# Sums of squares of the norms over 1024 features added up on GpSimd instead of by matrix products

## The chip, the cores and the metric

The kernel runs on one core of one Trainium2 chip. The metric is the device time of one execution in microseconds (us). The kernel before took 1709.74 us, the median of three runs (1708.4 to 1711.4).

## The reference, cut to what matters

Two transformer blocks follow each other on 256 latent tokens with 1024 features, beside 256 context tokens. Every normalisation over the 1024 features divides a token by the root of its mean square, and is followed by a scale and a shift:

```python
def rms_norm(x, g):
    xf = x.astype(jnp.float32)
    y = xf * lax.rsqrt(jnp.mean(xf * xf, axis=-1, keepdims=True) + NORM_EPS)
    return (y * g.astype(jnp.float32)).astype(x.dtype)

for i in range(DEPTH):                                      # DEPTH = 2
    h_lat = modulate(rms_norm(x, norm_mix[i]), sh1, sc1)
    h_ctx = modulate(rms_norm(ctx, norm_mix[i]), csh1, csc1)
    ...                                                     # attention (i = 0) or latent attention (i = 1)
    x = x + g1 * y_lat
    x = x + g2 * squared_relu_mlp(modulate(rms_norm(x, norm_mlp[i]), sh2, sc2), mlp_w1[i], mlp_w2[i])
    if not last:                                            # the same for ctx
        ...
# second block
h = modulate_2(x, norm1_g[layer], sh1, sc1)                 # rms norm, scale, shift
...                                                         # gated delta rule, convolution, Fourier mix
x = x + g1 * mix
x = x + g2 * swiglu(modulate_2(x, norm2_g[layer], sh2, sc2), w_ffn_in[layer], w_ffn_out[layer])
return rmsnorm(x, final_g)
```

Everything is float32. The kernel makes eight such sums of squares over 256 tokens and one over 512 (latent and context together).

## The kernel before

**Tiling.** The latent `xl` and the context `xc` are kept transposed: 128 features on the partitions, 8 chunks of features (`KD`), 256 tokens. A product in full precision is three matrix products of split operands (`mm3`, lines 297 to 299: high by high, low by high, high by low). The weights come in blocks from DRAM on SP's queue, and each block is cut in two parts, `wh` on ScalarE (line 185) and `wl` on VectorE (line 186).

**Sum of squares.** Where a stage makes the last update of `x`, chunk by chunk, it also adds up the squares. `stat_open` clears a PSUM bank `part`. For chunk c, `stat_add` squares [128, 256] into `sq` (GpSimd, line 357; at the start of the kernel ScalarE, line 359). For the chunks 0 to 6 a product of `sq` with a [128, 32] matrix of ones adds the sum over the partitions into one of four strips of 32 rows of `part` (line 362). After chunk 6, VectorE copies `part` to `partS` (line 369), and small products with a selecting column (line 371) turn its strips into sums by token, in columns. Chunk 7 goes straight to the columns (line 365). Then VectorE scales the sum (`rq_m`, line 308), GpSimd raises it to the power of -0.5 (`rs`, line 310), and TensorE spreads `rs` over the partitions by a product (`R`, line 407 or 388). VectorE and ScalarE make the next stage's input `hh`, `hl` from `x` and `R` (lines 394 to 397).

**The places**, in order of time: the inputs (x and ctx); the last quarter of layer 0's out-projection, for the latent (`lat_norm`) and for the context; the end of layer 0's MLP (512 tokens wide, latent and context together); the end of layer 1's latent attention (`mla_out`); the end of layer 1's MLP; the end of the second block's mixing (`mix_out`); and the end of its MLP, before the output.

**Order.** Python generators emit the stages woven into each other (the out-projection of layer 0 beside attention, the context's delta rule beside layer 1), and a scheduler then puts each engine's instructions into one fixed order. The start of the kernel alone is in an order written out by hand. Each engine works through its own list, so an instruction that waits holds up all that is behind it on its engine.

Of the kernel before, what the change touches and what calls it, by code (L numbers as in the profile page):

```python
# [7 lines left out]
F32 = mybir.dt.float32  # L8
F32R = mybir.dt.float32r
I32 = mybir.dt.int32  # L10
AF = mybir.ActivationFunctionType
# [3 lines left out]
P = 128  # L15
# [25 lines left out]
def _const_arrays():  # L41
# [9 lines left out]
    sel = np.where(np.arange(128)[:, None] % 32 == 0, 1.0, 0.0).astype(np.float32)  # L51
    c1 = np.concatenate([ident, np.repeat(sel, 2, 1), np.ones((128, 32), np.float32), m0, m1, mb, _rope(64), _rope(32)], 1)
# [21 lines left out]
for _n, _w in (("ident", 128), ("sel", 2), ("ones", 32), ("m0", 128), ("m1", 128), ("mb", 64), ("rope64", 256), ("rope32", 128)):  # L74
    _C1[_n] = (_o, _o + _w)
    _o += _w
# [9 lines left out]
class Blank:  # L86
    """Stands for everything while the order of the weight blocks is recorded."""
# [17 lines left out]
class Split:  # L105
    """A float32 operand as two float32r parts: hi + lo is the value exactly."""
# [109 lines left out]
class Part:  # L216
    """Keys, queries and values of the delta rule on 256 tokens of the latent or the context."""
# [17 lines left out]
class Build:  # L235
# [9 lines left out]
    # -- debugging taps --  # L245
# [4 lines left out]
    # -- filler: work of the tensor engine that nothing waits for yet --  # L250
# [43 lines left out]
    # -- small pieces --  # L294
# [9 lines left out]
    def rsqrt_steps(self, out, ss, n, scale, eps=EPS):  # L304
        """out = (ss * scale + eps) ** -0.5 on [128, n]."""
# [7 lines left out]
    def cut(self, dst, src, scale=None):  # L313
        """dst.hi + dst.lo = src * scale, scale per partition."""
# [14 lines left out]
    def filled(self, gen):  # L329
        """Runs a generator, with as much filler as it yields."""  # L330
        for u in gen:
            self.fill(u)

    def stat_open(self, tag, n, bufs=2):
        """Begins the sums of squares of n halves of 256 tokens; column 2 r + t for token tile t of half r."""
        pool = self.ps_s if tag == "s" else self.ps_t
        part = pool.tile([P, 512], F32, tag=tag, name="part", bufs=bufs)
        self.nc.vector.memset(part, 0.0)
        if n == 1:
            ms = part[:, 256:260]  # L340
        else:
            ms = pool.tile([P, 4], F32, tag=tag, name="ms", bufs=bufs)
            self.nc.vector.memset(ms, 0.0)
        self.stat = (part, ms, n)
        return self.stat

    def stat_add(self, c, r=None, x=None, stat=None, sqp=None):
        """Adds chunk c of x (half r or both); the last one goes straight to the columns."""
        nc = self.nc
        part, ms, n = stat or self.stat  # L350
        rs = range(n) if r is None else (r,)
        f = slice(256 * rs[0], 256 * rs[-1] + 256)
        sq = sqp.tile([P, 256], F32, tag="sqf", name="sq", bufs=4) if sqp else self.tmp.tile([P, 512], F32, tag="sq", name="sq")
# [877 lines left out]
    def residual(self, c, ps, T, mod, g, last=False, r=None):  # L1231
# [4 lines left out]
        if last:  # L1236
            self.stat_add(c, r)
# [1021 lines left out]
```

## Time and profile before

| | before |
|---|---|
| median of 3 runs | 1709.74 us (1708.4 to 1711.4) |
| span of the profiled execution | 1706.0 us |
| TensorE busy | 1655.3 us, 97% of the span, 12256 products |
| VectorE busy | 1130.2 us, 66% |
| ScalarE busy | 715.1 us, 42% |
| GpSimd busy | 218.4 us, 13% |
| DMA moved | 257.31 MB, 151 GB/s on average |

The profiled execution has no device time of its own on record; its span is 3.7 us below the median of the runs. The busy shares are means over stages of different kinds. What a change is worth in a stage is read from that stage: from the order of the instructions in time, from how dense each engine is there, and from which wait ends last.

### The profile page before, as it was taken

How to read it: one execution, taken by the hardware profiler on the slowest of the kernel's cores; microseconds unless marked ns; L12 is line 12 of the kernel's file. 1: busy time of each engine (PE TensorE's matmuls, PEld its weight loads, DVE VectorE, ACT ScalarE, POOL GpSimd, SP SyncE). 2: the span in 40 equal slices, each digit the busy share in tenths (PEclk: the TensorE clock that was granted, in tenths of full speed). 3: DMA queues.
4: the chain of work that ended last, by engine and by line, in shares of the span. 5: the costliest groups of instructions: out<-in, count | busy, mean ns of one | idle time of the engine just before them, and what ended most of it. 6: DMA issues, size and time to landing. Idle time of an engine off the chain costs nothing.

```text
span 1706.0 us, 30446 instructions
## 1 busy us (share of the span) xinstructions
PE 1655.3 (97%) x12256; PEld 1405.4 (82%) x12256; DVE 1130.2 (66%) x2156; ACT 715.1 (42%) x1336; POOL 218.4 (13%) x294
## 2 busy tenths in 40 slices
PE   7999999999999999998999999999999999999998
PEld 5676687687877787666667999998989999899997
DVE  3575856667767776558777885675865856665643
ACT  3344443332332323147664644443533435444442
POOL 1430132110000000225321100101020000100000
PEclk8999999999999999999999999999999999999999
DMA  9684254225567777573222454454423545545652
GB/s 339 210 230 126 53 58 72 54 83 185 179 210 239 243 245 221 161 232 107 67 58 64 147 163 146 152 172 116 139 73 112 157 132 159 173 139 184 185 168 81
DMA packets 193229, 257.31 MB, mean 151 GB/s; under 512 B 9263, under 2 KB 166816, under 8 KB 193088
## 3 DMA queue, kind: packets, MB, share of 16 engines
q1 hardware_dynamic: 189488, 248.29, 46.1%
q0 software_dynamic: 2016, 2.33, 3.0%
q10 hardware_dynamic: 1584, 4.74, 0.8%
q8 instruction: 96, 1.57, 0.4%
q14 instruction: 45, 0.37, 0.1%
HBM read 254.28 MB, written 1.05 MB: 150 GB/s over the span
## 4 chain that ended last, share of the span: by engine, by line
PE 89%; DMA 4%; ACT 2%; DVE 2%; issue 1%; POOL 1%; POOLq 0%; DVEq 0%; SPq 0%; ACTq 0%
PE m L297 11%; PE m L299 11%; PE m L298 11%; PE ov L1091 3%; PE pf L297 3%; PE pf L298 3%; PE pf L299 3%; PE ip L297 2%; PE ip L298 2%; PE ip L299 2%; PE pps L1077 2%; PE adaps L508 2%; PE part L362 2%; PE ml L1534 1%; PE pg L299 1%; PE pg L297 1%
## 5 line engine op out<-in xcount | busy, mean ns | idle before, releaser
L185 ACT ACTIVATE wh<-wr 128x1024 fp32r<-128x1024 f32 (+3 forms) x354 | 332.2, 984 | 420.9 <-PE m L298 189.9
L186 DVE TENSOR_TENSOR wl<-wr,wh 128x1024 fp32r<-128x1024 f32 (+3 forms) x354 | 402.2, 1164 | 146.6 <-ACT wh L185 145.9
L299 PE MATMUL m<-hh,wl 128*128 128x256 f32 (+1 forms) x544 | 177.5, 329 | 0.5 <-DVE wl L186 0.5
L297 PE MATMUL m<-hh,wh 128*128 128x256 f32 (+1 forms) x544 | 176.7, 330 | 1.1 <-ACT hh L395 1.1
L298 PE MATMUL m<-hl,wh 128*128 128x256 f32 (+1 forms) x544 | 177.1, 328 | 0.0
L297 PE MATMUL m<-hidh,wh 128*128 128x512 f32 (+1 forms) x512 | 173.6, 341 | 0.0
L298 PE MATMUL m<-hidl,wh 128*128 128x512 f32 (+1 forms) x512 | 172.6, 338 | 0.0
L299 PE MATMUL m<-hidh,wl 128*128 128x512 f32 (+1 forms) x512 | 172.6, 338 | 0.0
L357 POOL TENSOR_TENSOR sq<-xl 128x256 f32<-128x256 f32 x48 | 31.6, 662 | 721.1 <-DVE xl L1234 692.5
L299 PEld LDWEIGHTS m<-hh,wl 128*128 128x128 f32 x544 | 103.3, 190 | 11.6 <-issue 1.9
L297 PEld LDWEIGHTS m<-hh,wh 128*128 128x128 f32 x544 | 102.3, 190 | 12.6 <-issue 1.9
L298 PEld LDWEIGHTS m<-hl,wh 128*128 128x128 f32 x544 | 103.4, 190 | 9.5 <-issue 0.8
L297 PEld LDWEIGHTS m<-hidh,wh 128*128 128x128 f32 x512 | 96.7, 190 | 15.5 <-issue 3.8
L298 PEld LDWEIGHTS m<-hidl,wh 128*128 128x128 f32 x512 | 97.1, 190 | 14.6 <-issue 4.8
L299 PEld LDWEIGHTS m<-hidh,wl 128*128 128x128 f32 x512 | 96.9, 189 | 13.3 <-issue 3.3
L297 PE MATMUL pf<-hfh,wh 128*128 128x256 f32 x352 | 99.5, 287 | 1.1 <-ACT hfh L395 1.1
L298 PE MATMUL pf<-hfl,wh 128*128 128x256 f32 x352 | 100.0, 285 | 0.0
L299 PE MATMUL pf<-hfh,wl 128*128 128x256 f32 x352 | 100.0, 285 | 0.0
L297 PE MATMUL ip<-wh,hh 128*128 128x256 f32 x288 | 86.2, 301 | 0.0
L298 PE MATMUL ip<-wl,hh 128*128 128x256 f32 x288 | 84.6, 294 | 0.2 <-DVE wl L186 0.2
L299 PE MATMUL ip<-wh,hl 128*128 128x256 f32 x288 | 83.6, 290 | 0.0
L1234 DVE SCALAR_TENSOR_TENSOR xl<-m,mod,xl 128x256 f32<-128x256 f32 x64 | 30.6, 481 | 74.3 <-PE m L299 74.2
(592 smaller groups left out, 4185.2 us busy)
## 6 DMA issues: line engine op xcount, KB each, us to landing
wr<-in_mlp_w SPq DMA_DIRECT2D x128, 512.0 KB, 4.6
av<-in_ada_w SPq DMA_DIRECT2D x48, 512.0 KB, 4.0
wr<-in_w_ffn_in SPq DMA_DIRECT2D x44, 512.0 KB, 4.6
wr<-in_w_in SPq DMA_DIRECT2D x42, 512.0 KB, 4.4
wr<-in_ada_w SPq DMA_DIRECT2D x32, 512.0 KB, 6.2
av<-in_w_mod SPq DMA_DIRECT2D x32, 512.0 KB, 4.1
wr<-in_w_gate SPq DMA_DIRECT2D x24, 512.0 KB, 4.6
wf<-in_ada_w SPq DMA_DIRECT2D x16, 512.0 KB, 11.6
```

Source lines behind the costliest of these rows:

```text
L185: b.nc.scalar.activation(out=hi[:, o + a:o + z], in_=t[:, a:z], func=AF.Copy)
L186: b.nc.vector.tensor_tensor(out=lo[:, o + a:o + z], in0=t[:, a:z], in1=hi[:, o + a:o + z], op=ALU.subtract)
L297: mm(ps, l.hi, r.hi, start=start, stop=False, **kw)
L298: mm(ps, l.hi, r.lo, start=False, stop=False, **kw)
L299: mm(ps, l.lo, r.hi, start=False, stop=stop, **kw)
L357: nc.gpsimd.tensor_tensor(out=d, in0=v, in1=v, op=ALU.mult)
L362: nc.tensor.matmul(part[j:j + 32, f], self.c1("ones"), sq[:, f], start=False, stop=c >= 3, skip_group_check=True)
L508: nc.tensor.matmul(ps[32 * j:32 * j + 32, :], S[:, k, :], m, start=k == 0, stop=k == KD - 1, skip_group_check=True)
L1077: nc.tensor.transpose(ps[:, o:o + P], pt[:, qt, k0:k0 + P], self.ident)
L1091: self.nc.tensor.matmul(o[64 * f:64 * f + 64, 0:256], vals(f, kt), T[f][:, kt, :], start=kt == 0, stop=kt == nk - 1, skip_group_check=True)
L1234: self.nc.vector.scalar_tensor_tensor(x, ps[:, 256 * i:256 * i + 256], mod[:, i, 8 * g + c:8 * g + c + 1], x, op0=ALU.mult, op1=ALU.add)
L1534: self.nc.tensor.matmul(s, q[:, i, t * P:t * P + P], k[:, i], start=True, stop=True)
```

## The change

All sums of squares over 1024 features are formed without the products of line 362.

- Each half has an accumulator `sqa` [128, 256] in SBUF. Chunk 0 is squared straight into it; the chunks 1 to 6 are squared into `sq` and added to `sqa` by GpSimd. Chunk 7 is squared into `sq`. Then two products per token tile with a column of ones, one of `sqa` and one of `sq`, give the sums by token. The clearing of PSUM, the copy `partS` and the selecting column go. The PSUM bank is taken only at chunk 7.
- The squares run on ScalarE in the out-projection of layer 0 (latent and context) and in `mla_out` (`act=True`), and on GpSimd in the three MLPs and in `mix_out`.
- For the two inputs, ScalarE squares the rows of tokens as they came from DRAM, 512 features at a time, and sums them along the row in the same instruction; VectorE adds the two halves of a row.
- Beside that, the constants lose the two columns of `sel`, the tiles of vectors are as wide as what they hold, and two small tiles of the latent attention share the tags of others.

```diff
-    def stat_open(self, tag, n, bufs=2):
-        pool = self.ps_s if tag == "s" else self.ps_t
-        part = pool.tile([P, 512], F32, tag=tag, name="part", bufs=bufs)
-        self.nc.vector.memset(part, 0.0)
...
+    def stat_open(self, tag, n, bufs=2, pool=None):
+        acc = [(p or self.tmp).tile([P, 256], F32, tag="sqa", name="sqa", bufs=1) for p in (None, pool)[:n]]
+        self.stat = {"tag": tag, "n": n, "bufs": bufs, "acc": acc, "ps": None}
         return self.stat
 
-    def stat_add(self, c, r=None, x=None, stat=None, sqp=None):
+    def stat_add(self, c, r=None, x=None, stat=None, act=False):
...
+        sq = None if c == 0 else self.tmp.tile([P, 512], F32, tag="sq", name="sq")
+        part = {r: acc[r] if c == 0 else sq[:, 256 * r:256 * r + 256] for r in rs}
         for r in rs:
-            v, d = (x or self.x[r])[:, c], sq[:, 256 * r:256 * r + 256]
-            if True and not sqp:
-                nc.gpsimd.tensor_tensor(out=d, in0=v, in1=v, op=ALU.mult)
+            v = (x or self.x[r])[:, c]
+            if act:
+                nc.scalar.activation(out=part[r], in_=v, func=AF.Square)
             else:
-                nc.scalar.activation(out=d, in_=v, func=AF.Square)
-        if c < KD - 1:
-            j = 32 * (c % 4)
-            nc.tensor.matmul(part[j:j + 32, f], self.c1("ones"), sq[:, f], start=False, stop=c >= 3, skip_group_check=True)
-        else:
+                nc.gpsimd.tensor_tensor(out=part[r], in0=v, in1=v, op=ALU.mult)
+            if 0 < c < KD - 1:
+                nc.gpsimd.tensor_tensor(out=acc[r], in0=acc[r], in1=part[r], op=ALU.add)
+        if c == KD - 1:
+            if st["ps"] is None:
+                pool = self.ps_s if st["tag"] == "s" else self.ps_t
+                st["ps"] = pool.tile([P, 512], F32, tag=st["tag"], name="part", bufs=st["bufs"])
+                st["ms"] = st["ps"][:, 256:260]
             for t in range(2 * rs[0], 2 * rs[-1] + 2):
-                nc.tensor.matmul(ms[:, t:t + 1], sq[:, t * P:t * P + P], self.c1("ones")[:, 0:1],
-                                 start=False, stop=True, skip_group_check=True)
-        if c == KD - 2:
-            sq = self.tmp.tile([P, 512], F32, tag="nm", name="partS")
-            nc.vector.tensor_copy(sq[:, f], part[:, f])
-            for t in range(2 * rs[0], 2 * rs[-1] + 2):
-                nc.tensor.matmul(ms[:, t:t + 1], sq[:, t * P:t * P + P], self.c1("sel")[:, 0:1],
-                                 start=False, stop=True, skip_group_check=True)
+                for i, y in enumerate((acc[t // 2], part[t // 2])):
+                    nc.tensor.matmul(st["ms"][:, t:t + 1], y[:, t % 2 * P:t % 2 * P + P], self.c1("ones")[:, 0:1],
+                                     start=i == 0, stop=i == 1)
...
         def tokens(i):
-            self.stats[i] = self.stat_open("s", 1)
             yield from self.load_T(self.x[i], xt[i])
-            for c in range(KD):
-                self.stat_add(c, 0, self.x[i], self.stats[i], self.wfirst)
-                yield 1.0
-            yield from self.half_R(i, R, self.stats[i])
+            ss = self.small.tile([P, 2, 2], F32, tag="nt", name="nt")
+            ms = self.small.tile([P, 2], F32, tag="nr", name="nr")
+            for q in range(2):
+                for t in range(2):
+                    sq = self.tmp.tile([P, 512], F32, tag="sq", name="sq")
+                    nc.scalar.activation(out=sq, in_=xt[i][t][:, 512 * q:512 * q + 512], func=AF.Square,
+                                         accum_out=ss[:, q, t:t + 1])
+                    yield 1.0
+                    if q and t:
+                        nc.vector.tensor_tensor(out=ms, in0=ss[:, 0], in1=ss[:, 1], op=ALU.add)
+                    yield 1.0
+            yield from self.half_R(i, R, {"ps": None, "ms": ms})
...
-            self.stat_add(c, 0, self.x[r], stat)
+            self.stat_add(c, 0, self.x[r], stat, True)
...
-                    self.stat_open(*(("s", 2) if l == 0 else ("fil", 1, 1)))
+                    self.stat_open(*(("s", 2, 2, mp) if l == 0 else ("fil", 1, 1)))
...
-            self.residual(c, ps, 256, self.mod1, 2, gr == 3)
+            self.residual(c, ps, 256, self.mod1, 2, gr == 3, act=True)
```

**Where the order of the instructions moves.** A row is one instruction, or a run of like ones, of one engine in its fixed order: line, operation, output and inputs, shape, count.

TensorE in layer 0's out-projection for the latent, at its end (`pps` turns the attention's weights, ScalarE copies them to `PT`, `ov` multiplies them with the values, `op` is the out-projection); before:

```order
L1077 MATMUL pps<-cst_81,Pm 128x128 x4
L1091 MATMUL ov<-PT,vB 64x256 x4
L362 MATMUL part<-sq,cst_81 32x256 x2
L1091 MATMUL ov<-PT,vB 64x256
L297 MATMUL op<-OTh,wh 128x256
L362 MATMUL part<-sq,cst_81 32x256
L1091 MATMUL ov<-PT,vB 64x256 x3
```

and after:

```order
L1076 MATMUL pps<-cst_81,Pm 128x128 x4
L1090 MATMUL ov<-PT,vB 64x256 x5
L296 MATMUL op<-OTh,wh 128x256
L363 MATMUL part<-cst_81,sqa 128x1
L1090 MATMUL ov<-PT,vB 64x256 x3
```

The two products with ones that stood between the fourth and the fifth product with `PT` are gone, and nothing stands in their place.

TensorE at the entry of layer 1 (`adaps` are products of the modulation, with weights just read from DRAM; `ms` are the columns of sums; `cq` is the first product that needs the norm); before:

```order
L508 MATMUL adaps<-wr,S_6421 32x512 x3
L362 MATMUL part<-sq,cst_81 32x512
L508 MATMUL adaps<-wr,S_6421 32x512 x3
L371 MATMUL ms<-cst_81,partS 128x1 x4
L365 MATMUL ms<-cst_81,sq 128x1 x2
L508 MATMUL adaps<-wr,S_6421 32x512 x2
L365 MATMUL ms<-cst_81,sq 128x1 x2
L508 MATMUL adaps<-wr,S_6421 32x512 x2
L407 MATMUL R<-cst_81,rs 128x128 x4
L508 MATMUL adaps<-wr,S_6421 32x512 x4
L297 MATMUL cq<-wh,hh 128x384
```

and after:

```order
L501 MATMUL adaps<-wr,S_6376 32x512 x6
L363 MATMUL part<-cst_81,sqa 128x1
L363 MATMUL part<-cst_81,sq 128x1
L363 MATMUL part<-cst_81,sqa 128x1
L363 MATMUL part<-cst_81,sq 128x1
L363 MATMUL part<-cst_81,sqa 128x1
L363 MATMUL part<-cst_81,sq 128x1
L363 MATMUL part<-cst_81,sqa 128x1
L363 MATMUL part<-cst_81,sq 128x1
L501 MATMUL adaps<-wr,S_6376 32x512 x6
L400 MATMUL R<-cst_81,rs 128x128 x4
L501 MATMUL adaps<-wr,S_6376 32x512 x2
```

All eight column products now stand ahead of the `adaps` that follow the first six, and six `adaps` instead of four stand between the first six and `R`.

VectorE at the end of `mix_out` (`xl` is the last update of x, `wl` the cut of the next weights, `nm` the first step that needs `R`); before:

```order
L1234 SCALAR_TENSOR_TENSOR xl<-wo,mod_116,xl 128x256 x2
L369 COPY partS<-part 128x256
L186 TENSOR_TENSOR wl<-wr,wh 128x1024
L308 TENSOR_SCALAR rq_m<-part 128x2
L186 TENSOR_TENSOR wl<-wr,wh 128x1024
L394 SCALAR_TENSOR_TENSOR nm<-xl,Af,R 128x256 x2
```

and after:

```order
L1233 SCALAR_TENSOR_TENSOR xl<-wo,mod_116,xl 128x256 x2
L185 TENSOR_TENSOR wl<-wr,wh 128x1024 x2
L307 TENSOR_SCALAR rq_m<-part 128x2
L387 SCALAR_TENSOR_TENSOR nm<-xl,Af,R 128x256 x2
```

`rq_m` now stands behind both cuts of weights, where one of them stood behind it before; the same holds at the entry of the second block.

## Rows read from the trace of the kernel before

**Rows 1.** Page, busy time of each engine, share of the span, instructions.

```profile
PE 1655.3 (97%) x12256; PEld 1405.4 (82%) x12256; DVE 1130.2 (66%) x2156; ACT 715.1 (42%) x1336; POOL 218.4 (13%) x294
```

**Rows 2.** Page, chain of work that ended last, by line.

```profile
PE m L297 11%; PE m L299 11%; PE m L298 11%; PE ov L1091 3%; PE pf L297 3%; PE pf L298 3%; PE pf L299 3%; PE ip L297 2%; PE ip L298 2%; PE ip L299 2%; PE pps L1077 2%; PE adaps L508 2%; PE part L362 2%; PE ml L1534 1%; PE pg L299 1%; PE pg L297 1%
```

**Rows 3.** Line 362, its products: count, then duration in ns, smallest, median, largest.

```profile
L362 PE MATMUL part<-sq,cst x126: 379/379/617, 12.5 to 1696.7; 128*32 128x256 f32 x112, 128*32 128x512 f32 x14
```

**Rows 4.** Timeline, PE, final MLP: start, duration, line, operation, count, [idle before, releaser].

```profile
1681.42 0.28 PE L298 MATMUL po<-hidl,wh 128*128 128x256 f32 x1
1681.63 0.62 PE L362 MATMUL part<-sq,cst 128*32 128x256 f32 x2
1682.18 0.38 PE L299 MATMUL po<-hidh,wl 128*128 128x256 f32 x1
1682.41 0.28 PE L297 MATMUL po<-hidh,wh 128*128 128x256 f32 x1
1682.53 0.28 PE L298 MATMUL po<-hidl,wh 128*128 128x256 f32 x1
```

**Rows 5.** Timeline, PE, last quarter of layer 0's MLP, 512 tokens wide.

```profile
718.01 0.39 PE L297 MATMUL m<-hidh,wh 128*128 128x512 f32 x1
718.33 1.04 PE L362 MATMUL part<-sq,cst 128*32 128x512 f32 x2
719.30 0.50 PE L298 MATMUL m<-hidl,wh 128*128 128x512 f32 x1
719.64 0.39 PE L299 MATMUL m<-hidh,wl 128*128 128x512 f32 x1
719.87 0.39 PE L297 MATMUL m<-hidh,wh 128*128 128x512 f32 x1
```

**Rows 6.** Timeline, PE, end of layer 0's out-projection for the latent.

```profile
332.17 0.63 PE L362 MATMUL part<-sq,cst 128*32 128x256 f32 x4
332.98 0.65 PE L1091 MATMUL ov<-PT,vB 128*64 128x256 f32 x2 [0.18 <-ACT PT L1082]
```

**Rows 7.** Windows: start:end, length, busy of PE, PEld, DVE, ACT, POOL, clock, DMA.

```profile
337.00:345.00 8.00, 8.00 (x59) 6.37 (x59) 6.82 (x17) 2.46 (x5) 3.74 (x6) 1.00 0.30 111
926.00:952.00 26.00, 24.46 (x206) 23.96 (x204) 23.96 (x61) 16.38 (x29) 3.30 (x3) 1.00 0.58 176
24.00:34.00 10.00, 7.61 (x38) 6.38 (x38) 7.06 (x19) 3.95 (x8) 0.69 (x1) 0.54 1.05 384
```

**Rows 8.** Timeline, PE, first product that needs the context's norm after the out-projection.

```profile
360.93 0.74 PE L297 MATMUL m<-hh,wh 128*128 128x256 f32 x4 [1.11 <-ACT hh L395]
```

**Rows 9.** Line 357, GpSimd's squares of the latent.

```profile
L357 POOL TENSOR_TENSOR sq<-xl x48: 608/612/1525, 323.6 to 1697.0; 128x256 f32<-128x256 f32 x48
```

**Rows 10.** Line 1173, GpSimd's sum of two tiles 512 wide.

```profile
L1173 POOL TENSOR_TENSOR bm<-bm,cst x8: 1082/1086/1107, 126.1 to 305.2; 128x512 f32<-128x512 f32 x8
```

**Rows 11.** Timeline, DVE and POOL, out-projection of the context.

```profile
344.67 2.16 POOL L357 TENSOR_TENSOR sq<-xc 128x256 f32<-128x256 f32 x2 [1.55 <-DVE xc L1227]
345.05 1.32 DVE L186 TENSOR_TENSOR wl<-wr,wh 128x1024 fp32r<-128x1024 f32 x1
347.04 1.21 DVE L186 TENSOR_TENSOR wl<-wr,wh 128x1024 fp32r<-128x1024 f32 x1
```

**Rows 12.** Timeline, PE, entry of layer 1.

```profile
729.87 1.05 PE L508 MATMUL adaps<-wr,S 128*32 128x512 f32 x4 [0.87 <-DMA wr<-in_w_mod]
...
733.24 1.90 PE L407 MATMUL R<-cst,rs 128*128 128x128 f32 x8
735.07 1.15 PE L508 MATMUL adaps<-wr,S 128*32 128x512 f32 x8
```

**Rows 13.** Timeline, end of mix_out.

```profile
1492.40 0.42 DVE L369 COPY partS<-part 128x256 f32<-128x256 f32 x1
...
1494.26 1.61 POOL L310 TENSOR_TENSOR rs<-rq_m,neghalf 128x2 f32<-128x2 f32 x1 [1.23 <-DVE rq_m L308]
```

**Rows 14.** Line 310, GpSimd's power of the norms' sums; duration in ns, smallest, median, largest.

```profile
L310 POOL TENSOR_TENSOR rs<-rq_m,neghalf x9: 695/714/1609, 19.7 to 1699.1; 128x2 f32<-128x2 f32 x8, 128x4 f32<-128x4 f32 x1
```

More of the change, by code (lines that the diff above doesn't have):

```diff
@@ L50, in _const_arrays @@
     mb = np.where((kc >= c0) & (kc < c0 + 16), 0.0, NEG).astype(np.float32)
-    sel = np.where(np.arange(128)[:, None] % 32 == 0, 1.0, 0.0).astype(np.float32)
-    c1 = np.concatenate([ident, np.repeat(sel, 2, 1), np.ones((128, 32), np.float32), m0, m1, mb, _rope(64), _rope(32)], 1)
+    c1 = np.concatenate([ident, np.ones((128, 32), np.float32), m0, m1, mb, _rope(64), _rope(32)], 1)
     le = (i <= j).astype(np.float32)
@@ L73 @@
 _o = 0
-for _n, _w in (("ident", 128), ("sel", 2), ("ones", 32), ("m0", 128), ("m1", 128), ("mb", 64), ("rope64", 256), ("rope32", 128)):
+for _n, _w in (("ident", 128), ("ones", 32), ("m0", 128), ("m1", 128), ("mb", 64), ("rope64", 256), ("rope32", 128)):
     _C1[_n] = (_o, _o + _w)
@@ L377, in stat_close @@
+    def stat_close(self):
+        n = 2 * self.stat["n"]
         rs = self.small.tile([P, 4], F32, tag="rs", name="rs")
-        a, z = (0, 2 * n) if r is None else (2 * r, 2 * r + 2)
-        self.rsqrt(rs[:, a:z], ms[:, a:z], z - a, 1.0 / D)
+        self.rsqrt(rs[:, :n], self.stat["ms"][:, :n], n, 1.0 / D)
         return rs
@@ L384, in half_R @@
         rs = self.small.tile([P, 4], F32, tag="rs", name="rs")
-        yield from self.rsqrt_steps(rs[:, 0:2], stat[1][:, 0:2], 2, 1.0 / D)
-        R[r] = stat[0][:, :256]
+        yield from self.rsqrt_steps(rs[:, 0:2], stat["ms"][:, 0:2], 2, 1.0 / D)
+        if stat["ps"] is None:
+            stat["ps"] = self.ps_s.tile([P, 512], F32, tag="s", name="part")
+        R[r] = stat["ps"][:, :256]
         for t in range(2):
@@ L399, in norm_R @@
     def norm_R(self, R):
-        n = 2 * self.stat[2]
+        n = 2 * self.stat["n"]
         yield 2.0
@@ L480, in turn @@
             nc.tensor.transpose(ps[:, :o], t[:o], self.ident[:o, :o])
-            d = self.const.tile([P, P], F32, name="vec" + rows[0][0])
-            nc.vector.tensor_copy(d[:, :o], ps[:, :o])
+            d = self.const.tile([P, o], F32, name="vec" + rows[0][0])
+            nc.vector.tensor_copy(d, ps[:, :o])
             for k, (a, z) in at.items():
@@ L673, in pair @@
                     yield 0.2
-        self.stats = {}
         with st, self.tc.manual_schedule():
@@ L1227, in outproj3, with residual @@
             self.nc.vector.scalar_tensor_tensor(x, ps, self.mod0[:, r, 16 + c:17 + c], x, op0=ALU.mult, op1=ALU.add)
-            self.stat_add(c, 0, self.x[r], stat)
+            self.stat_add(c, 0, self.x[r], stat, True)
             yield 0.7
-    def residual(self, c, ps, T, mod, g, last=False, r=None):
+    def residual(self, c, ps, T, mod, g, last=False, r=None, act=False):
         for i in range(T // 256) if r is None else (r,):
@@ L1236, in residual @@
         if last:
-            self.stat_add(c, r)
+            self.stat_add(c, r, act=act)
     def mlp(self, l, T, mod, head=None):
@@ L1494, in mla_heads @@
         kt = []
-        ss = self.small.tile([P, 4, 4], F32, tag="vs", name="vs")
-        rs = self.small.tile([P, 4, 4], F32, tag="vr", name="vr")
+        ss = self.small.tile([P, 4, 4], F32, tag="hn", name="vs")
+        rs = self.small.tile([P, 4, 4], F32, tag="hr", name="vr")
         for t in range(4):
```

13 lines of the change are left out of this document (2 added, 11 removed).

## The prediction

> **What bounds the kernel now.** I read the page first: TensorE is busy for 97% of the span and no other engine for more than 66% [rows 1]. The chain of waits followed back from the end runs mostly through products, and names line 362, the products with ones, with 2% of the span, about 34 us [rows 2]. So the removed products lie on the path, not beside it. The line's own view counts them: 126 records, two to a product, so 63 products: 56 over 256 tokens (seven in each of eight halves) and seven over 512 [rows 3]. What remains is what one of them costs in its stage, what becomes late in its place, and what the new work on ScalarE and GpSimd holds up.
>
> **The price of a product.** The timeline of the final MLP shows one in a dense stream. From the start of the product before it (1681.42) to the second product behind it (1682.41) pass 0.99 us; two steps of that stream are 2 x 0.12 = 0.24 [rows 4]. It costs 0.75 us, more than its own 0.62, since the products around it are spread. In the MLP 512 tokens wide, 718.01 to 719.64 is 1.63, less two steps of 0.23: 1.17 us [rows 5].
>
> **The sum, stage by stage**, on the clock of the profiled execution. Of the seven products of an MLP or of mix_out the seventh stands behind the last product of the stage, where the path runs through the last update of x and not through TensorE, so I count six there.
>
> *The inputs: 0.* 14 products go, but from 24 to 34 us the DMA engines are full (share 1.05) at half the clock, 0.54 [rows 7]: the first weights set the pace. The squares were ScalarE's before. Bounds: a loss of 1.5, if fewer products leave the clock low earlier (of that row's 7.61 us of products, some 3 us more at 1.2 instead of 2.4 GHz), and a gain of 2.
>
> *Out-projection, latent: 3.8.* Seven products are 5.3. But two of them stood between the products that wait for the attention's transposed weights: they end just before a product that still waits 0.18 us for the copy PT [rows 6]. In the new order nothing stands there, so that wait grows by what they filled, and two of the seven give nothing: 5 x 0.75 = 3.8. Bounds 3.0 and 5.3. The squares move to ScalarE, 31% busy in the next window [rows 7].
>
> *Out-projection, context: 5.3.* 7 x 0.75; TensorE has no gap there, 8.00 of 8.00 us [rows 7]. VectorE, at 6.82, is the next that could bind; the 1.1 us wait for this norm [rows 8] may go, since the sums stand earlier. I set these two against each other. Bounds 3.0 and 6.4.
>
> *MLP of layer 0: 7.8.* Six at 1.17 are 7.0. At the entry of layer 1, R started at 733.24, and the product that waits for weights from DRAM at 729.87 [rows 12]. Now all column products are ahead of that wait, so the norm is no longer late, and R waits for six adaps instead of four products with two columns and the late norm between. Four adaps take 1.15 us [rows 12]: six take 1.7, or 3.5 at half clock. R starts at 731.6 to 733.3, 0 to 1.6 earlier; I take 0.8. Bounds 6.0 and 9.5.
>
> *mla_out: 3.0.* 5.3 at full price. But behind it, from 926 to 952, VectorE is busy for 23.96 of 26 us, about as long as TensorE with 24.46 [rows 7]: products that come earlier wait there for cuts and for the convolution. The edit takes only a clearing and a copy from VectorE (0.42 for the copy, [rows 13]). I take a little over half. Bounds 1.0 and 5.3.
>
> *MLP of layer 1, mix_out, final MLP: 4.5 each, 13.5.* Six at 0.75. At the ends of the first two, rq_m falls behind a second cut of weights, 1.21 us [rows 11]. Against that, the copy of 0.42 is gone, and the power, which took 1.61 us beside that cut [rows 13], stands clear of it at 0.70 [rows 14]: 1.21 - 0.42 - 0.91 = -0.1, so R comes when it came. Bounds 3.5 and 5.3 each (the final one: 4.0 and 5.2).
>
> *New work.* GpSimd gets 48 additions of two tiles [128, 256]. The trace has none; the nearest rows are its square of that shape, 0.61 [rows 9], and its sum of tiles twice as wide, 1.08 [rows 10], so 0.54 to 0.61 us. In the three halves whose squares move to ScalarE one addition replaces one square, so GpSimd's load stays. In the others it does two operations a chunk, 1.2 us, where a chunk of an MLP's quarter or of mix_out is 24 products of 0.12 us [rows 4], 2.9 us; so only chunk 6's addition is near the end of a stage, and it is over before chunk 7 is there to be squared. I cost it at nothing. If that cover were gone, one addition, 0.6 us, would be added at each of four ends, inside the bounds.
>
> Sum: 0 + 3.8 + 5.3 + 7.8 + 3.0 + 13.5 = 33.4 us, the profiled span 1706.0 becoming 1672.6. The span is 3.7 us below the median of the runs; with that the time is 1709.74 - 33.4 = **1676.3 us**. The low bounds sum to -1.5 + 3.0 + 3.0 + 6.0 + 1.0 + 3.5 + 3.5 + 4.0 = 22.5 (1687.2), the high ones to 2 + 5.3 + 6.4 + 9.5 + 5.3 + 5.3 + 5.3 + 5.2 = 44.3 (1665.4).
>
> **Rivals.**
>
> *A. The woven halves give nothing.* In the two out-projections and in mla_out other engines take over as the bound: VectorE's 6.82 of 8 and 23.96 of 26 us speak for it [rows 7], the gapless 8.00 of 8 of TensorE against. Then 33.4 - 3.8 - 5.3 - 3.0 = 21.3 us are gained: 1688.4.
>
> *B. All comes out.* 42 products (all but the inputs') at 0.75 and seven at 1.17 are 31.5 + 8.2 = 39.7, and with the layer's entry (1.6), the context's wait (1.1) and the inputs (2) 44.4: 1665.3. The chain's 34 us for line 362, the inputs' products included [rows 2], speaks against most of it.
>
> *C. Slower, by GpSimd in VectorE's way.* Beside one cut wl, two squares took 2.16 us instead of 1.22, and the cut 1.32 instead of 1.21 [rows 11]. If an addition stretched to 1.08 held a cut that TensorE waits for by its whole length, 48 additions would cost 52 us and the kernel would take 1709.74 - 33.4 + 52 = 1728. It decides from 33.4 / 48 = 0.70 us per addition. Against it: of the two engines GpSimd is the one that was stretched, by 0.94, while the cut lost 0.11; 48 x 0.11 is 5 us if TensorE waited for each of them, and in dense stretches like [rows 4] it waits for none. The Trainium skill, "SBUF — State Buffer", section "Who interferes with whom", speaks against this change: GpSimd and VectorE share a port pair as an exclusive lock for a whole instruction, and the one that issues second blocks fully. The long squares agree with VectorE having been first; that rows show no cut blocked for a whole square agrees less. By that rule with every addition first, at 0.61 each, an estimate is 48 x 0.61 = 29 us lost, 1706: a gain of 4 left.
>
> *D. The products go but their time does not.* The order shows the 63 products gone and nothing of like size put in, so only waits could take it all: new ones of 33 us. Nothing in the profile names them.
>
> **How the numbers follow.** Forecast 0.67, A 0.14, B 0.11, C 0.05, D 0.03. About 0.2% (3.4 us) is what a measurement of this kernel can tell from no change. Forecast, A and B are faster by more: 0.92. D is within: 0.03. C is slower: 0.05. The range takes the forecast's bounds and the cases A and B: 1665 to 1689.
>
> **What would show it right or wrong.** The profile after should have no products with 32 columns of ones; TensorE's busy time should fall by about 35 us, with its share still near 97%. Between the places named, stretches should keep their length. Out-projection of the latent: a wait for PT of about 0.8 us. Entry of layer 1: R 1.7 to 3.5 us behind the product that waits for weights from DRAM, with its sums long there. Ends of layer 1's MLP and of mix_out: a power of 0.70 us with nothing beside it, and R as far behind the last product as before. From 926 to 952: if the norm of mla_out ends as long before the wait for the keys' norm as now, rival A holds there. GpSimd: additions near 0.6, up to 1.1 beside cuts. The prediction is wrong if VectorE's cuts become longer by some tenths throughout (C), if the first 40 us stretch by more than 2 us, or if the layers' entries show new waits for GpSimd's last addition.

## The result, and the profile after

The changed kernel takes **1685.86 us** (median of four runs, 1684.99 to 1686.62). Its ratio to the kernel before is 0.986, 95% interval 0.985 to 0.988: about 24 us faster, where the forecast was 33.4. The time lies inside the range of 1665 to 1689. The profiled span went from 1706.0 to 1683.2 us, by 22.8.

The page's busy times (beside [rows 1]): TensorE lost 30.9 us of busy time, where about 35 was forecast, and holds the same share, 97%; VectorE's time did not move; GpSimd got 37 us more.

```profile
PE 1624.4 (97%) x12114; PEld 1395.5 (83%) x12114; DVE 1131.8 (67%) x2139; ACT 723.3 (43%) x1360; POOL 255.3 (15%) x318
```

GpSimd's additions (line 355) and its powers (line 309; beside [rows 14]), durations in ns, smallest, median, largest:

```profile
L355 POOL TENSOR_TENSOR sqa<-sqa,sq x48: 723/743/1720, 325.2 to 1672.6; 128x256 f32<-128x256 f32 x48
...
L309 POOL TENSOR_TENSOR rs<-rq_m,neghalf x9: 696/707/1032, 16.5 to 1675.9; 128x2 f32<-128x2 f32 x8, 128x4 f32<-128x4 f32 x1
```

An addition takes 0.74 us by the median, and 17 of the 48 took 1.07 to 1.72 us; 0.54 to 0.61, and up to 1.1, was forecast. To see where the time went, take a VectorE instruction that both kernels have and read its start in both timelines: the difference is the gain up to there, and two such differences enclose a stage. The table holds such pairs.

| Up to | Start before | Start after | Gain so far | Of this stage | Forecast |
|---|---|---|---|---|---|
| end of layer 0's attention | 315.53 | 315.85 | -0.3 | -0.3 | 0 |
| out-projection, latent, to its norm's sum | 337.10 | 333.05 | 4.05 | 4.4 | 3.8 |
| out-projection, context | 427.58 | 417.93 | 9.65 | 5.6 | 5.3 |
| MLP of layer 0, body | 686.70 | 680.05 | 6.65 | **-3.0** | 0 |
| MLP of layer 0, end | 724.86 | 711.90 | 12.96 | 6.3 | 7.0 |
| entry of layer 1 | 789.55 | 777.82 | 11.73 | **-1.2** | 0.8 |
| mla_out | 987.81 | 976.23 | 11.58 | **-0.15** | 3.0 |
| MLP of layer 1 | 1217.21 | 1201.49 | 15.7 | 4.1 | 4.5 |
| opening of the second block | 1267.38 | 1253.12 | 14.3 | **-1.5** | 0 |
| mix_out | 1639.78 | 1621.27 | 18.5 | 4.2 | 4.5 |
| final MLP | 1694.29 | 1671.31 | 23.0 | 4.5 | 4.5 |

Wherever products were taken out of a dense stream, the forecast's size came. The missing 10.6 us lie mostly in the four bold rows: two stages in which the change removes nothing, and two in which the removed products had stood in waits.

**Where it went as forecast.** TensorE's timeline at the end of the latent's out-projection (beside [rows 6]): the wait for PT grew from 0.18 to 0.68 us.

```profile
329.58 0.65 PE L1090 MATMUL ov<-PT,vB 128*64 128x256 f32 x2 [0.68 <-ACT PT L1081]
```

GpSimd's and TensorE's timelines at the end of mix_out (beside [rows 13]): the power stands alone at 0.71 us, and R starts 4.30 us behind the last update of x, 4.07 before, because the norm's sum is read behind two cuts of weights now.

```profile
1476.67 0.71 POOL L309 TENSOR_TENSOR rs<-rq_m,neghalf 128x2 f32<-128x2 f32 x1 [2.36 <-DVE rq_m L307]
```
```profile
1477.43 0.71 PE L400 MATMUL R<-cst,rs 128*128 128x128 f32 x4 [2.24 <-POOL rs L309]
```

**mla_out.** Windows of this stage (columns as in [rows 7]): TensorE is idle for 1.5 of 6 us, and then the granted clock is 0.50 for 4 us and 0.77 for five more. Before, the stage's 15 us from 911 to 926 were all busy, at 1.00. The windows of before come first.

```profile
911.00:918.00 7.00, 7.00 (x52) 5.53 (x51) 6.13 (x14) 1.83 (x5) 1.84 (x3) 1.00 0.00 0
918.00:926.00 8.00, 8.00 (x46) 4.90 (x44) 5.04 (x12) 2.00 (x5) 2.53 (x4) 1.00 0.01 3
```

```profile
906.00:912.00 6.00, 4.50 (x27) 3.32 (x25) 4.83 (x9) 3.01 (x7) 2.30 (x4) 0.96 0.00 0
912.00:916.00 4.00, 3.87 (x19) 3.85 (x19) 3.77 (x6) 3.07 (x6) 0.00 (x0) 0.50 0.35 67
916.00:921.00 5.00, 5.00 (x36) 5.00 (x35) 2.00 (x6) 1.05 (x4) 0.00 (x0) 0.77 1.06 354
```

**Entry of layer 1.** TensorE's timeline (beside [rows 12]): two transfers of weights, not one, are waited for ahead of R; the four products of 717.00 (x8: two records to a product) run at half clock; and a third wait follows R.

```profile
717.00 3.19 PE L501 MATMUL adaps<-wr,S 128*32 128x512 f32 x8 [1.42 <-DMA wr<-in_w_mod]
721.14 1.05 PE L501 MATMUL adaps<-wr,S 128*32 128x512 f32 x4 [0.95 <-DMA wr<-in_w_mod]
722.12 1.16 PE L400 MATMUL R<-cst,rs 128*128 128x128 f32 x8
725.00 1.05 PE L501 MATMUL adaps<-wr,S 128*32 128x512 f32 x4 [1.72 <-DMA wr<-in_w_mod]
725.98 0.44 PE L296 MATMUL cq<-wh,hh 128*128 128x384 f32 x1
```

**Opening of the second block.** VectorE's, GpSimd's and TensorE's timelines, one after the other. The scheduler put vT ahead of A on VectorE; vT waited 0.54 us for si and then took 1.09 us (0.42 before), since GpSimd's AT, begun at 1224.44, held it up until 1227.82; and TensorE waited 1.61 us for E, which stands behind them. This wait is in all the kernels with the change. No run took it apart, so the reading of it as the cause of this stage's loss is argued from the rows alone.

```profile
1227.02 1.09 DVE L1679 SCALAR_TENSOR_TENSOR vT<-si,cv 128x256 f32<-128x256 f32 x1 [0.54 <-ACT si L1678]
1228.04 1.11 DVE L1832 SCALAR_TENSOR_TENSOR A<-kkp,bf,A 128x128 f32<-128x128 f32 x4
```
```profile
1224.44 3.38 POOL L1824 TENSOR_TENSOR AT<-AT,cst 128x1024 f32<-128x1024 f32 x1
```
```profile
1236.74 1.13 PE L1847 MATMUL Abp<-E,cst 128*128 128x512 f32 x2 [1.61 <-DVE E L1844]
```

### The profile page after: what moved, and what is told of

Read it like the earlier page. It is cut to its first block, busy times and chain, and to the rows that moved or that the text cites. A ratio compares the mean times of both kernels' runs of the same rounds, so it can differ in the third digit from the quotient of the medians.

```text
span 1683.2 us, 30197 instructions
## 1 busy us (share of the span) xinstructions
PE 1624.4 (97%) x12114; PEld 1395.5 (83%) x12114; DVE 1131.8 (67%) x2139; ACT 723.3 (43%) x1360; POOL 255.3 (15%) x318
## 4 chain that ended last, share of the span: by engine, by line
PE 87%; DMA 5%; DVE 4%; ACT 2%; issue 1%; POOL 1%; SPq 0%; POOLq 0%; DVEq 0%; ACTq 0%
PE m L296 10%; PE m L298 10%; PE m L297 10%; PE ov L1090 3%; PE pf L296 3%; PE pf L297 3%; PE pf L298 3%; PE ip L296 2%; PE ip L297 2%; PE ip L298 2%; PE pps L1076 2%; PE adaps L501 2%; PE ml L1533 2%; PE pg L298 1%; PE pg L296 1%; PE pg L297 1%
## 5 line engine op out<-in xcount | busy, mean ns | idle before, releaser
L185 DVE TENSOR_TENSOR wl<-wr,wh 128x1024 fp32r<-128x1024 f32 (+3 forms) x354 | 408.6, 1181 | 144.9 <-ACT wh L184 144.4
L544 DVE SCALAR_TENSOR_TENSOR acc<-av,S,acc 128x1024 f32<-128x1024 f32 x56 | 70.7, 1280 | 13.7 <-DMA av<-in_ada_w 13.5
```

Of the source, the lines that this page charges most:

```text
L185: b.nc.vector.tensor_tensor(out=lo[:, o + a:o + z], in0=t[:, a:z], in1=hi[:, o + a:o + z], op=ALU.subtract)
L544: op = eng.scalar_tensor_tensor(d, w, s, d, op0=ALU.mult, op1=ALU.add)
```

## The experiments

Each run stands beside runs of the kernel before on the same chip, so ratios are compared rather than times where two kernels ran in different groups. Stages are measured as in the table, by pairs of starts.

### The body of layer 0's MLP: where tiles lie

The change drops two columns (8 bytes a partition) from a constant tile, and the tiles allocated behind it start 32 bytes earlier. Two kernels move them alone. The first adds two unused columns to the changed kernel, which puts them back:

```diff
-    c1 = np.concatenate([ident, np.ones((128, 32), np.float32), m0, m1, mb, _rope(64), _rope(32)], 1)
+    c1 = np.concatenate([ident, np.ones((128, 32), np.float32), np.zeros((128, 2), np.float32), m0, m1, mb, _rope(64), _rope(32)], 1)
...
-for _n, _w in (("ident", 128), ("ones", 32), ("m0", 128), ("m1", 128), ("mb", 64), ("rope64", 256), ("rope32", 128)):
+for _n, _w in (("ident", 128), ("ones", 32), ("pad", 2), ("m0", 128), ("m1", 128), ("mb", 64), ("rope64", 256), ("rope32", 128)):
```

> The changed kernel with two columns of zeros put back into the table of constants (8 bytes a partition, which the allocator rounds to 32), so that every tile behind it lies on the same multiple of 64 bytes as in the kernel before; the order of the instructions of TensorE, VectorE and GpSimd is the same as in the changed kernel. Theory (placement): in the changed kernel's layer-0 MLP the products that read h step 0.233 us apart where they stepped 0.227 before, because the tiles moved by 32 bytes; here they step 0.227 again, about 3 us come back between 410 and 680 us, and the time is about 1682.7. Rival (something else of the change slows them, the order or GpSimd beside them): the steps stay at 0.233 and the time at 1685.9.

The second does the same to the kernel before with eight columns, 32 bytes, and changes nothing else; its order of instructions is that of the kernel before.

> The kernel before with eight columns of zeros more in the table of constants, so that all tiles behind it move by 32 bytes, onto the multiples of 64 that they have in the changed kernel; nothing else is changed. Placement: the products that read h in layer 0's MLP step 0.233 us apart instead of 0.227, and the time is about 3 us above 1709.7, some 1713. Rival: steps of 0.227 and 1709.7.

Groups by line and shape in the middle of this MLP (count, busy us, mean ns of one): before, before moved by 32 bytes, after, and after put back. The first line of each pair reads the MLP's input hh, the second the hidden tile.

```profile
L297 PE MATMUL m<-hh,wh 128*128 128x512 f32 x192 | 75.1, 391 | 0.0
...
L297 PE MATMUL m<-hidh,wh 128*128 128x512 f32 x194 | 76.1, 392 | 0.0
```
```profile
L297 PE MATMUL m<-hh,wh 128*128 128x512 f32 x192 | 76.3, 397 | 0.0
L297 PE MATMUL m<-hidh,wh 128*128 128x512 f32 x190 | 74.5, 392 | 0.0
```
```profile
L296 PE MATMUL m<-hh,wh 128*128 128x512 f32 x192 | 76.1, 396 | 0.0
...
L296 PE MATMUL m<-hidh,wh 128*128 128x512 f32 x193 | 75.5, 391 | 0.0
```
```profile
L296 PE MATMUL m<-hidh,wh 128*128 128x512 f32 x199 | 77.8, 391 | 0.0
...
L296 PE MATMUL m<-hh,wh 128*128 128x512 f32 x192 | 75.1, 391 | 0.0
```

A product that reads hh (or hl) takes 5 ns longer in the second and third kernel, and returns to 391 in the fourth; one that reads the hidden tile stays. There are 576 of the former (m from hh and wh, from hh and wl, from hl and wh, 192 each; hl is what the upper half hh leaves over): 576 x 5 ns is 2.9 us, and the stage lost 3.0 after the change, 3.0 in the moved kernel before, and nothing in the one put back (a gain of 7.8 going in, 8.1 coming out). In the eight profiles of kernels with the tiles moved the stage lost 2.9 to 3.0 us; in the four of padded changed kernels it gave between 0.0 and 0.7. So 32 bytes of placement is the cause. In the total time it is not resolved by these two runs: the moved kernel before took 1711.69 us beside 1713.05, ratio 0.9996 [0.998, 1.001], and the padded one 1685.04 us, ratio 0.9845 [0.983, 0.986] beside 0.986, both within the scatter.

Why the padded kernel's profile did not gain the 3 us in all lies at two other places. At the entry of layer 1 it lost 3.0 us, where the changed kernel lost 1.2. The other is seen in the windows of the out-projection, after and then padded: the low clock that follows the wait for the attention ended by 318 in one execution, and lasted into the next window in the other, which cost 2 us there. From 318 to 324 the granted clock was 0.73, 0.80 and 0.79 in three of the four padded kernels and 1.00 in the fourth, 0.83 in one kernel without padding and 0.90 to 1.00 in the rest; whether the placement has a part in it is open.

```profile
312.00:318.00 6.00, 5.19 (x30) 3.90 (x30) 3.66 (x12) 3.41 (x12) 0.00 (x0) 0.72 0.31 87
318.00:324.00 6.00, 6.00 (x46) 5.03 (x43) 4.70 (x16) 3.20 (x13) 0.00 (x0) 1.00 0.00 0
```
```profile
312.00:318.00 6.00, 5.78 (x28) 4.58 (x29) 3.32 (x10) 2.91 (x10) 0.00 (x0) 0.50 0.28 85
318.00:324.00 6.00, 6.00 (x33) 3.99 (x30) 3.54 (x12) 1.65 (x7) 0.00 (x0) 0.73 0.00 0
```

### mla_out: ScalarE, or waits that products had filled

Two theories stood. By one, the squares that the change puts on ScalarE hold up what ScalarE writes for TensorE there. This run leaves them on GpSimd:

```diff
-            self.residual(c, ps, 256, self.mod1, 2, gr == 3, act=True)
+            self.residual(c, ps, 256, self.mod1, 2, gr == 3)
```

> The changed kernel with the squares of mla_out on GpSimd again, as before, additions as in the change. Theory (ScalarE in the way): the squares stand between the cuts hch of the context's input on ScalarE; the product ba waits for hch and hcl (1.0 us in three waits near 907), TensorE idles 1.5 us of six, its clock falls to half from 912 to 918, and so the gain of this half is lost. Here these waits and the half clock go, and 2 to 3 us come back: about 1683. Rival (the removed products themselves had filled the time in which TensorE waits for the context's input, wherever the squares are made): idle time and half clock stay, 1686, or somewhat above if GpSimd with two operations a chunk makes the sum late.

Ratio 0.9856 [0.984, 0.987], 1686.83 us, as the change itself; the stage gave 0.2. Its windows show the same wait and the same fall of the clock, so ScalarE is not the cause:

```profile
906.00:912.00 6.00, 4.99 (x36) 4.16 (x34) 5.87 (x13) 1.67 (x4) 5.84 (x9) 1.00 0.00 0
912.00:916.00 4.00, 3.35 (x16) 2.97 (x16) 2.82 (x3) 2.56 (x4) 1.85 (x3) 0.54 0.00 0
```

By the other, the removed products had filled time in which TensorE waits, and kept its clock. This run puts seven products with ones back where they stood; nothing reads their result, and the norm is still made by the additions:

```diff
+            if c < KD - 1 and "idle" in st: nc.tensor.matmul(st["idle"][:32, :256], self.c1("ones"), part[r], start=True, stop=True, skip_group_check=True)
...
-            self.stat_open("s", 1)
+            self.stat_open("s", 1)["idle"] = self.ps_s.tile([P, 512], F32, tag="s", name="idle", bufs=2)
```

> The changed kernel with the seven products with ones of mla_out put back as well, their result unused (the sums still come from the additions). At the price of a dense stream they cost 7 x 0.75 = 5.3 us: 1691. If they only fill time in which TensorE waits and keep its clock up (the rival of e3), they cost nothing or gain: 1684 to 1686, with the clock near full from 912 to 918. If ScalarE's squares are the cause, the waits for hch and hcl stay and the time is 1688 to 1691.

```profile
906.00:912.00 6.00, 6.00 (x39) 4.15 (x38) 3.07 (x7) 3.02 (x7) 2.92 (x4) 1.00 0.00 0
912.00:916.00 4.00, 4.00 (x34) 3.96 (x34) 3.94 (x6) 3.36 (x6) 0.00 (x0) 1.00 0.35 81
```

TensorE is busy throughout at the full clock, 34 products pass from 912 to 916 where 19 did, and the stage gives 1.7 us. In the total time this run alone shows no gain: 1683.53 us, ratio 0.984 [0.982, 0.986], within the scatter of the changed kernel. The same with the tiles put back gave 1679.93, ratio 0.9805 [0.978, 0.983], and in a second run 1681.66, 0.982 [0.980, 0.984]:

> Both repairs in one: the changed kernel with the padded table of constants and the idle products in mla_out. If the two effects are independent, the layer-0 MLP keeps its steps of 0.227 (3 us) and mla_out its clock (2 to 3 us): 1680 to 1681, faster than both kernels. If the clock's fall depends on other things as well (it fell at one place of one execution for no reason that the order gives), 1682 to 1685.

> The padded table of constants and the idle products in mla_out, beside the changed kernel: 1680, 5 to 6 us below it, if both effects hold from one execution to the next; 2 to 3 below it if only one does.

Over all profiles the stage gave 1.7 to 3.3 us in the four with the unused products, and -1.2 to 0.2 in the six without (the additions on VectorE, below, left aside: -3.3). A single profile of this stage says little: e2 and e12, which keep the order of before here, show 1.7 and -3.2. The clock says more: it falls to 0.50 to 0.54 at this place in all seven profiles of changed kernels without the unused products, and in none of the four with them and the three with the order of before. In a stage that waits, seven products not only cost nothing: putting them back gained 2 to 3 us. GpSimd's additions hold up some of the cuts hcl there (0.91 and 0.95 us instead of 0.42), which TensorE waits for; with the additions on VectorE every hcl took 0.42, and TensorE still waited (0.80, 0.62 and 0.51 us) and fell to 0.50, from 918 to 920, so this is not the cause either. The changed kernel, run beside the last of them, kept both its own time and this window, 4.45 of 6 us busy and then 4 us at 0.50:

> The changed kernel once more, as the reference for the three beside it: 1685 to 1687. In a second profile the clock is at half near 912 to 918 again if the missing products are the cause there, and the products that read h in layer 0's MLP step 0.233 us apart again.

1685.15 us, ratio 0.984 [0.982, 0.986]: the padded kernel with unused products is 3.5 us below it on the same chip, where 5 to 6 was forecast if both effects hold and 2 to 3 if one does. The intervals of the two ratios overlap; of the times themselves, 1677.9 to 1683.9 and 1684.0 to 1685.7, none of one kernel reaches into the other's.

### The entry of layer 1

R stands behind products with weights from DRAM (adaps). This run gives R the bank that those use, so that the ones still to come stand behind R:

```diff
-        R[0] = self.ps_t.tile([P, 512], F32, tag="t", name="R")
+        R[0] = self.ps_t.tile([P, 512], F32, tag="fil", name="R", bufs=1) if n == 4 else self.ps_t.tile([P, 512], F32, tag="t", name="R")
```

> The changed kernel, with R of layer 1's entry in the PSUM bank that the adaps products use, so that all of these come behind the norm instead of ahead of R. Theory (adaps in the way): in the changed kernel R starts at 722.1, 5.2 us after its rs is done at 717.0, since six adaps stand ahead of it and wait twice for weights from DRAM (1.4 and 1.0 us), the four between at half clock. Here R starts within 0.5 us of rs, and 2 to 4 us are gained at cq; part of it is given back later, where the adaps stand in the stream of products (16 of them at some 0.3 us, 5 us less what they fill). Time 1683 to 1686. Rival (the weights from DRAM bound this entry whatever the order): cq starts no earlier relative to the last product of the MLP, 1686 to 1688.

R came at 718.04 instead of 722.12, and the gain stood 3.6 us higher at 740; by 790 all of it and 12 us more were gone. The weights' products, 4.0 us of waiting for DRAM among them, now stood alone behind it. 1696.78, ratio 0.991 [0.989, 0.993], is above both forecasts, 1683 to 1686 and 1686 to 1688. The waits for weights move with the order; they don't go.

The next run, on the padded kernel with the unused products, fills the wait instead: six more unused products with ones behind the column products.

```diff
         rs = self.stat_close()
+        for i in range(6 if n == 4 else 0): self.nc.tensor.matmul(self.stat["ps"][:32, 0:256], self.c1("ones"), self.stat["acc"][i % 2], start=True, stop=True, skip_group_check=True)
```

> The same with six products with ones, result unused, behind the column products at layer 1's entry; they also change the order there, to two adaps instead of six between the columns and R. Theory (the adaps that wait for weights stand in the way of R, and TensorE loses its clock while it waits): R starts 2 to 3 us earlier relative to the last product of the MLP, and, unlike in e5, the adaps follow at once behind R: 1677 to 1679. Rival (what R gains, cq loses again to the adaps behind it): 1680.

```profile
712.33 1.02 PE L502 MATMUL adaps<-wr,S 128*32 128x512 f32 x2 [1.42 <-DMA wr<-in_w_mod]
...
713.16 3.65 PE L397 MATMUL part<-sqa,cst 128*32 128x256 f32 x10
716.74 1.16 PE L401 MATMUL R<-cst,rs 128*128 128x128 f32 x8
717.83 0.64 PE L502 MATMUL adaps<-wr,S 128*32 128x512 f32 x4
```

Two products with weights (four records) stand ahead of R instead of six, one wait for DRAM is left, and the stage gives 1.5 us; it lost 2.9 in the same kernel without the six products, in one profile each. The time is **1674.83 us**, ratio 0.979 [0.976, 0.981], below both kernels, below the forecast of 1677 to 1679 and, with an interval that doesn't touch that of the changed kernel beside it, about 10 us faster. What the six products do is two things at once, a filled wait and another order around R; one run does not split them.

### The price in a dense stream, GpSimd's part, the inputs

Unused products put back in mix_out and the final MLP, seven each, by the line shown for mla_out:

> The changed kernel with seven products with ones, result unused, put back in mix_out and in the final MLP, where TensorE runs without a gap. The forecast's price for a product in a dense stream is 0.75 us, for six of each seven: 9.0 us, 1694.9. Rival (a product with ones costs its own time of 0.62 or less, and what the change gained here has another source, such as the clearing and the copy): 7 us or less, under 1693. Set beside the same seven products in mla_out, which cost nothing.

1694.82 us, ratio 0.990 [0.988, 0.992], beside 0.986 and 0.984 for the changed kernel: 7 to 10 us longer. The profiles agree: mix_out gave 0.0 instead of 4.2, and the final MLP 1.2 instead of 4.5, together some 7.5, where six each at 0.75 us are 9.0. The total time alone does not decide between the two theories, since the rival's 7 us lie within it; the starts around the products do, which are 0.74 us further apart for each of the twelve. In the final MLP the new order also moved ten of the twelve records of the output's transposes out of the stream, some 1.1 us, which is why it lost only 3.3. So [rows 4] priced these stages right, and the same products that are free in mla_out cost their full price here.

The 48 additions on VectorE instead of GpSimd:

```diff
-                nc.gpsimd.tensor_tensor(out=acc[r], in0=acc[r], in1=part[r], op=ALU.add)
+                nc.vector.tensor_tensor(out=acc[r], in0=acc[r], in1=part[r], op=ALU.add)
```

> The changed kernel with its 48 additions on VectorE instead of GpSimd. Theory of the forecast (the additions on GpSimd are covered, and what VectorE loses to them is small): no gain; VectorE has 48 instructions more, at about 0.4 us some 20 us of its time, and in the woven halves, where it is busy for over 0.85 of the time, it loses up to 1 us each: 1686 to 1689. Rival (GpSimd and VectorE block each other, rival C of the forecast): VectorE's cuts near the sums become shorter, and the time falls below 1684.

One takes 0.42 us there, not 0.74, and yet the time is 1688.51, ratio 0.987 [0.985, 0.988], against 0.986 and 0.984 for the two runs of the change: not better, and 2.7 us longer by medians. VectorE's cuts did get shorter, 402.5 us in all instead of 408.6, but the time did not fall with them. In its trace the stretch of the two out-projections gives 6.5 us instead of 10.0, where VectorE had no time left ([rows 7]), and mla_out loses 3.3. Moving the additions to VectorE gains nothing.

The kernel before with only the inputs' sums of squares made the new way:

> The kernel before with the new sums of the two inputs alone (rows of tokens squared and summed on ScalarE, 14 products fewer). The forecast sets this part at 0, since the first weights from DRAM set the pace: the same time as before within 1.5 us, and the first 100 us as long as before within what executions differ by. Rival (the products removed there were on the path, or the clock falls earlier without them): 2 us or more to either side.

1713.14 beside 1711.01, ratio 1.001 [0.999, 1.002]: nothing beyond the interval, where at most 1.5 us was forecast.

## Why the prediction was right, and where it was not

**Right.** The price of a product from its place in the stream: 4.5 forecast and 4.5 found in the final MLP, 4.5 and 4.2 in mix_out, 4.5 and 4.1 in layer 1's MLP, 7.0 and 6.3 at the end of layer 0's; and the run that put them back took 4.2 of 4.2 away in mix_out and 3.3 of 4.5 in the final MLP. That layer 1's MLP came so close is in part luck: over the profiles it gave 4.1 to 5.9, and 5.7 in the second one of the same kernel, above the bound of 5.3. The latent's out-projection gave 4.4 for 3.8, with the wait for PT grown as the step said (0.68; 0.8 forecast). The context's gave 5.6 for 5.3: its wait of 1.1 us for hh in [rows 8] is gone, a gain that I had set against VectorE, and a new wait of 0.4 us, for the latent's norm, stands at 338.90. The inputs gave nothing that a run of their own resolves.

**mla_out, 3.0 forecast, 0 found: the step that failed.** I put the loss behind the stage, at VectorE from 926 to 952, and left the stage itself at the full price of a dense stream. The loss lies inside it. The gain stood at 15.4 us at 922.86 in the trace of before, and fell to 12.3 by 932.39: TensorE had run ahead, waited for hch, hcl and baT, and then worked at half clock. For the latent's out-projection I asked what would stand in the products' place between two waits; here I did not ask it and took the stage for a dense one; no row of the prediction shows it, [rows 7] begin at 926. Its windows were full in the kernel before because the removed products filled them. Rival A is therefore true of this stage only, and for another reason than the one it gave; the two out-projections gave their 10 us.

**The entry of layer 1, 0.8 forecast, -1.2 found.** The six products ahead of R were counted right. The step took from [rows 12] that one transfer is waited for; the path came 11 to 13 us earlier at that point, and the products with weights as well, 10.5 to 13.9 us. What the step missed is that two waits, 1.42 and 0.95 us, with half clock between them, now stand ahead of R, where one of 0.87 us stood before; they took more than the earlier sums gave. In the two kernels that remove nothing near this entry, the moved one and the one with the inputs alone, it lost 2.3 and 2.8 us, so its price in one execution is known to 2 or 3 us only; the dense stages of the same kernels repeat within 0.6.

**Two terms that were not in the sum.** The 3.0 us of the MLP's body come from an edit that I read and costed at nothing: the two columns dropped from the constants. The 1.5 us at the second block's opening come, by the rows alone, from an order that the scheduler changed far from the edit; I had looked at the order only in the stages that the change touches.

**GpSimd.** An addition takes 0.74 us by the median, above the 0.54 to 0.61 that was worked out from other operations, and up to 1.72 beside a cut, where 1.1 was the most expected; two operations a chunk still fit in the 2.9 us of a chunk. Rival C fell by its price: the kernel is faster, and moving the additions away from GpSimd gains nothing. Its mechanism is there. VectorE's and GpSimd's timelines in mix_out after the change:

```profile
1468.34 1.61 DVE L185 TENSOR_TENSOR wl<-wr,wh 128x1024 fp32r<-128x1024 f32 x1 [0.49 <-ACT wh L184]
1469.88 1.76 DVE L185 TENSOR_TENSOR wl<-wr,wh 128x1024 fp32r<-128x1024 f32 x1
```
```profile
1468.95 1.60 POOL L355 TENSOR_TENSOR sqa<-sqa,sq 128x256 f32<-128x256 f32 x1
```

Such a cut takes 1.22 us alone, and an addition 0.74. The addition of 1468.95 takes 0.86 us more, which is how long the cut before it still ran (to 1469.95) less 0.14; the cut of 1469.88 takes 0.54 more, which is what the addition still had (to 1470.55) less 0.13. All 27 cuts of this width that began while GpSimd worked on whole tiles are longer in this way, by up to 1.86 us, and 17 were in the trace of before; the pair of rows by which the prediction doubted it was one of the mild ones. The Trainium skill, "SBUF — State Buffer", section "Who interferes with whom", has the second of two such instructions blocked until the first is done, and the trace agrees. What failed is the prediction's estimate from it, a gain of 4 us left where the change kept 24: it charged every addition to the path in full. In sum VectorE's cuts became longer by 6.4 us only, 402.2 to 408.6 on the two pages, because the squares of before had blocked some of them too and at least 14 additions are themselves the second, held up by a cut; and moving the additions to VectorE took the 6 us of cuts back without making the kernel faster.

Added up: -3.0 and -1.5 that were not foreseen, -3.15 in mla_out, -2.0 at the entry, and -0.9 in the remaining stages together make the 10.6 us between 33.4 and 22.8. By the number alone rival A's 1688.4 is nearer to 1685.86 than the 1676.3 that was forecast, but A lost it at the out-projections, which came at full price, so its nearness is luck. That the time lies inside the range, near its upper end, owes as much to the width of the range as to the sum.

## What to carry to other kernels

Price a removed product from the starts around it, but only where the stream is dense without it; where it fills a wait, ask what TensorE will do instead, because it then waits and loses its clock, and unused work can be worth its place. Compare the addresses of all tiles and the order far from the edit as well as near it: a constant shortened by 8 bytes cost 3.0 us, and one exchanged pair of VectorE instructions, by the rows, 1.5. A stage that waits for weights from DRAM can give back what comes early. Work moved from TensorE to GpSimd takes turns with VectorE's cuts: price it by the cuts that the path waits for, not by the sum of all operations.

## What the hardware showed that was not expected

- **Placement by 32 bytes.** Moving the tiles by 32 bytes took a product 512 columns wide that reads hh or hl from 391 to 396 ns, and its step in the stream from 0.227 to 0.233 us. Products that read the hidden tile did not change. Which of the moved tiles does it (hh or the weights beside it) is open.
- **VectorE and GpSimd take turns.** In these traces a cut on VectorE (both operands in SBUF) that began while GpSimd worked on whole tiles, or the other way round, took longer by nearly all that the other still had to run: cuts of 1.22 us took up to 1.86 us more, additions of 0.74 us up to 0.98 more. VectorE's updates of x with an operand from PSUM (0.47 us) were not longer beside an addition, nor were cuts beside GpSimd's power.
- **The clock after a wait.** 1.5 us of idle time in six were followed by 4 us at 0.50, 1.2 GHz, and a slow recovery; unused products in that wait kept it at 1.00, 2.4 GHz. The Trainium skill, "TensorE: Matmul & The Clock Gate", section "HAM oscillation — how this bites in real kernels", tells of waits for transfers in a stream of products and of half speed behind them. Here the waits were for cuts of other engines, and the windows of mla_out show half speed behind them too. The low stretch from 312 on ends before 318 in some profiles and only after it in others, which is worth up to 2 us; why is open.
- **GpSimd's addition** of two tiles of 128 x 256 takes 0.74 us, more than its square of one such tile, 0.61.
